# Output-map products of an S5 layer moved from GpSimd to VectorE inside a hidden-layer MLP stage

## The chip, the cores and the metric

The kernel runs on one core of one Trainium2 chip. The time is the device time of one execution in microseconds (us); lower is better. The engines are TensorE (PE, with its weight loads as PEld), VectorE (DVE), ScalarE (ACT), GpSimd (POOL) and SyncE (SP), whose queue issues nearly all DMA transfers. Each engine takes its own instructions strictly in their order.

## The reference, cut to what matters

A sequence of 256 tokens of width 1024 runs through two blocks of two layers each, in float32. The first block ends with a stick-breaking attention and an MLP (`x + gate * relu(h w1)^2 w2`, hidden width 4096). The second block begins with an S5 layer, a diagonal state-space model in 64 groups of 16 channels with 64 complex states each:

```
lam_bar = jnp.exp(lam * dt)
b_bar = ((lam_bar - 1.0) / lam)[..., None] * b
bu = jnp.einsum('blgc,gpc->blgp', uf, b_bar)
_, states = lax.associative_scan(_ssm_binop, (a_elems, bu), axis=1)
y = jnp.real(jnp.einsum('blgp,gcp->blgc', states, c))
```

The kernel computes the S5 layer in pieces of 8 tokens. For that it needs, of each group of channels, an input map P (powers of `lam_bar` times `b_bar`), an output map K (powers of `lam_bar` times `c`) and a band of the local response (the product of the two). All three depend on the weights alone, and the kernel makes them on the chip before the S5 layer begins.

## The kernel before, in words

Weights are split into two parts that TensorE takes at full rate: ScalarE copies a 1 MB unit `raw` (128x2048) to `wh`, and VectorE writes `wl = raw - wh`. The splitting is done by `unit_ahead` (`act` is line 292, `tt` line 312), and two such units are needed for each step of an MLP.

The MLP of the first block's second layer (tag `m2`, the stage named mlp1 in the code) has 16 units of 256 hidden columns. Step u consists of `A(u)`, 48 matmuls that give hidden unit u in two PSUM banks, then VectorE's `wb` and `ht`, ScalarE's relu, square and `hh` copy, VectorE's `hl = ht - hh`, and of `B(u-1)`, 48 matmuls that multiply the unit before with w2. Banks 0 to 3 hold the output; the pairs 4, 5 and 6, 7 take turns for `A`.

Between these blocks the function `mlp` calls `sides(b)` twice a step: once behind `A(u)`, once behind `B(u-1)`. Each call advances three generators by a bit, and lends them the bank pair that `A` doesn't hold: `ada_side` (dot products for the modulation, line 668), `s5_turns` (angle tables, written to DRAM through SP) and `s5_pre2`, which makes the maps. `s5_pre2` treats 8 blocks b of 8 groups:

- `maps(b)`: three VectorE instructions of 128x1024 make P (`s5A`, with `tP` in `s5X` as scratch), three GpSimd instructions of 128x1152 (`gp`, line 1358) make K (`s5X`); then SP loads the coefficients of block b+2 (line 1357) and stores K (`dQ`).
- `turn(b, h)`, h = 0 and 1: TensorE turns four groups of P into the first lent bank, ScalarE copies it out (`s5X<-psall`), SP stores it (`dP`); four matmuls of P with K fill 128 columns of the second lent bank, which VectorE copies to `s5Kp` (line 1395). After h = 1 VectorE adds the diagonal to `s5Kp` and SP stores it in four pieces (`dK`).

The generator's order before is: one call with `maps(b)` and `turn(b-1, 0)`, the next with `turn(b-1, 1)` alone. The order of POOL and SP is the program's; the order of DVE, ACT and PE in this stage is set by a scheduler when the kernel is built. A matmul must wait until the bank that it writes has been emptied.

Of the kernel before, what the change touches and what calls it, by code (L numbers as in the profile page):

```python
# [10 lines left out]
F32 = mybir.dt.float32  # L11
F32R = mybir.dt.float32r
U8 = mybir.dt.uint8
AF = mybir.ActivationFunctionType
# [9 lines left out]
D = 1024  # L24
NK = D // 128
# [13 lines left out]

S5SEQ = "g P0 P1 g T0 T1 TB0 M0 P2 P3 TB1 Q0 Q1 T2 T3 g Q2 Q3"


# [227 lines left out]
class Prog:  # L272
# [122 lines left out]
    def unit_ahead(self, ahead, between=None):  # L395

        last = min(self.used_n + ahead, len(self.wseq) - 1)
        while self.split_n <= last:
            j = self.wseq[self.split_n]
            if j not in self.slot:  # L400
                assert self.split_n > self.used_n, ("not loaded", self.plan[j][1])
                break
            b = self.split_n % len(self.hb)
            raw = self.raw_of(j)
            n = 1 + (self.plan[j][1][0] in HALVES)
            parts = [slice(i * 2048 // n, (i + 1) * 2048 // n) for i in range(n)]
            for c in parts:
                self.act(self.hb[b][:, c], raw[:, c], AF.Copy)
            if between is not None:
                between()  # L410
                between = None
            for c in parts:
                self.tt(self.lb[b][:, c], raw[:, c], self.hb[b][:, c].bitcast(F32), SUB)
            self.release(j)
            self.split_n += 1
        if between is not None:
            between()
# [76 lines left out]
                wh, wl = (t[:, k, m * 128:(m + 1) * 128] for t in (hv, lv))  # L494
                self.pair(outs[m], wh, wl, self.X2[S][:, k], k == 0, k == NK - 1)

    def rows_mm(self, units, xs, banks, start, stop, evac=None):

        kt = [(h, l, j) for h, l in units for j in range(2)]
        out = lambda m: self.pb[banks[m // 2]][:, (m % 2) * T:(m % 2 + 1) * T]  # L500
        if evac is not None:
            fin, a, b = evac
        for m in range(NK):
            o = out(m)
            for q, (h, l, j) in enumerate(kt):
                c = j * D + m * 128
                xh, xl = xs[q]
                wh, wl = h[:, c:c + 128], l[:, c:c + 128]
                self.mm(o, wh, xh, q == 0 and start and m % 2 == 0, False)
                self.mm(o, wh, xl, False, False)  # L510
                self.mm(o, wl, xh, False, q == len(kt) - 1 and stop and m % 2 == 1)
            if evac is not None and m % 2 == 1:
                for i in (m - 1, m):
                    fin(i, out(i))
                    a(i)
                    if i:
                        b(i - 1)
        if evac is not None:
            b(NK - 1)
# [412 lines left out]
    def mlp(self, tag, S, finish, side=(), after=None, before=None):  # L932
        n = DFF // 256
        with self.tc.tile_pool(name="pm" + tag, bufs=1) as p:
            hh = [p.tile([128, 2, T], F32R, name=f"hh{i}") for i in range(3)]
            hl = [p.tile([128, 2, T], F32R, name=f"hl{i}") for i in range(3)]
            tt_ = [p.tile([128, 2, T], F32, name=f"ht{i}") for i in range(2)]
            wb = [p.tile([128, 2], F32, name=f"wb{i}") for i in range(2)]
            yb = (0, 1, 2, 3)

            def A(u):
                b = 4 + 2 * (u % 2)
                t = s = tt_[u % 2]
                ps = [self.pb[b], self.pb[b + 1]]
                self.proj_T((tag + "a", u), S, ps, n=258, parts=1 + (u == 0))
                if u == 0:
                    self.stats(6, std=True, r2=True)
                w = wb[u % 2]
                self.red(w, self.pball[:, b:b + 2, 256:258], ADD)
                for m in range(2):  # L950
                    self.stt(t[:, m, :], self.stdb, w[:, m:m + 1], ps[m][:, :T], MUL, ADD)
                self.act(t, t, AF.Relu)
                self.act(s, t, AF.Square)
                self.act(hh[u % 3], s, AF.Copy)
                self.tt(hl[u % 3], s, hh[u % 3].bitcast(F32), SUB)

            def B(us, fin=None):
                ws = [self.unit((tag + "b", u), ahead=2 - i) for i, u in enumerate(us)]
                xs = [(hh[u % 3][:, j, :], hl[u % 3][:, j, :]) for u in us for j in range(2)]
                self.rows_mm(ws, xs, yb, us[0] == 0, us[-1] == n - 1, fin)  # L960

            def sides(b):
                self.side_banks = (b, b + 1)
                for g, budget in side:
                    start = self.vcost
                    while next(g, "end") == "more" and self.vcost - start < budget:
                        pass

            A(0)
            for u in range(1, n - 1):  # L970
                A(u)
                sides(6 - 2 * (u % 2))
                if u == n - 2:
                    A(n - 1)
                B([u - 1])
                sides(4 + 2 * (u % 2))
            for g, _ in side:
                for _ in g:
                    pass
            if after is not None:  # L980
                after()
            if before is not None:
                before()
            B([n - 2, n - 1], finish)
# [348 lines left out]
    def s5_pre2(self):  # L1333

        nc = self.nc
        with self.tc.tile_pool(name="s5s", bufs=1) as p:
# [18 lines left out]
            dd = self.rsb.rearrange("p (g c) -> p g c", c=16)  # L1355
            nc.sync.dma_start(out=self.rsb, in_=self.a["s5d"])
            load = lambda b: nc.sync.dma_start(out=blk[b % 2], in_=self.a["s5blk"][b].rearrange("p a (s c) -> p a s c", c=16))
            gp = lambda out, a, b, op: nc.gpsimd.tensor_tensor(out=out, in0=a, in1=b, op=op)  # L1358
            nc.gpsimd.memset(Kp, 0.0)
            for i in range(2):  # L1360
                load(i)
            for _ in range(5):
                yield

            def maps(b):
                v, P, K = blk[b % 2], Pt[b % 2], Kt[b % 2]
                sl = slice(8 * b, 8 * b + 8)
                co = lambda i, k: v[:, i, :, None, :].to_broadcast([128, 8, k, 16])
                wv = lambda t, k: t[:, :, sl].rearrange("p d (s o) -> p s d o", o=1).to_broadcast([128, 8, k, 16])
                self.tt(P, co(0, 8), wv(WR, 8), MUL)  # L1370
                self.tt(tP, co(1, 8), wv(WI, 8), MUL)
                self.tt(P, P, tP, ADD)
                gp(K, co(2, 9), wv(X1, 9), MUL)
                gp(tK, co(3, 9), wv(X2, 9), MUL)
                gp(K, K, tK, ADD)
                if b < 6:
                    load(b + 2)
                nc.sync.dma_start(out=self.dram["Q"][b // 2][:, (b % 2) * 1024:(b % 2 + 1) * 1024]
                                  .rearrange("p (s x) -> p s x", x=128),
                                  in_=K[:, :, 1:9, :].rearrange("p s d c -> p s (d c)"))  # L1380

            def turn(b, h):
                P, K = Pt[b % 2], Kt[b % 2]
                b0, b1 = self.side_banks
                for s in range(4):
                    self.tr(self.pb[b0][:, s * 128:(s + 1) * 128], P[:, 4 * h + s, :, :].rearrange("p d c -> p (d c)"))
                self.act(Pu, self.pb[b0].rearrange("p (s x) -> p s x", x=128), AF.Copy)
                o = (b % 2) * 1024 + h * 512
                nc.sync.dma_start(out=self.dram["P"][b // 2][:, o:o + 512], in_=Pu.rearrange("p s x -> p (s x)"))
                for q in range(4):  # L1390
                    s = 4 * h + q
                    self.mm(self.pb[b1][32 * q:32 * q + 32, 0:128], P[:, s, 6:8, :].rearrange("p d c -> p (d c)"),
                            K[:, s, 0:8, :].rearrange("p d c -> p (d c)"))
                kp = Kp
                nc.vector.tensor_copy(out=kp[:, h, 112:240], in_=self.pb[b1][:, 0:128])
                if h:
                    self.tt(kp[:, :, 112:128], kp[:, :, 112:128], dd[:, 2 * b:2 * b + 2, :], ADD)
                    kd = self.dram["K"][:, b * 1920:(b + 1) * 1920].rearrange("p (g q x) -> p q g x", q=4, x=240)
                    for q in range(4):
                        nc.sync.dma_start(out=kd[:, q], in_=kp[32 * q + 16:32 * q + 32])  # L1400

            for b in range(9):
                if b < 8:
                    maps(b)
                if b:
                    turn(b - 1, 0)
                    yield
                    turn(b - 1, 1)
                yield

    def s5_turn(self, m):
# [394 lines left out]
```

## Time and profile before

| | |
|---|---|
| time, 3 runs | 1330.76 us median (1329.8 to 1332.6) |
| profiled execution | 1333.17 us |
| its span, first to last instruction | 1331.4 us |
| mean granted TensorE clock | 0.972 |
| stretch in which the maps are made | 514 to 681 us |

The profile is of a single execution. "Busy" is the time in which an engine has an instruction under way; a wait row names the engine and line that waited, and what ended the wait. Of the 1333.17 us, 1.77 us lie outside the span.

### The profile page before, as it was taken

How to read it: one execution, taken by the hardware profiler on the slowest of the kernel's cores; microseconds unless marked ns; L12 is line 12 of the kernel's file. 1: busy time of each engine (PE TensorE's matmuls, PEld its weight loads, DVE VectorE, ACT ScalarE, POOL GpSimd, SP SyncE). 2: the span in 40 equal slices, each digit the busy share in tenths (PEclk: the TensorE clock that was granted, in tenths of full speed). 3: DMA queues.
4: the chain of work that ended last, by engine and by line, in shares of the span. 5: the costliest groups of instructions: out<-in, count | busy, mean ns of one | idle time of the engine just before them, and what ended most of it. 6: DMA issues, size and time to landing. Idle time of an engine off the chain costs nothing.

```text
span 1331.4 us, 22520 instructions
## 1 busy us (share of the span) xinstructions
PE 1234.0 (93%) x9412; PEld 1144.7 (86%) x9412; DVE 1043.7 (78%) x1390; ACT 678.5 (51%) x868; POOL 169.2 (13%) x97
## 2 busy tenths in 40 slices
PE   2999999999999997977899789999999999999997
PEld 2999999999988897966889669887889999988886
DVE  6899999985999979898966856667656786877553
ACT  4545465554558855433455425544445555655442
POOL 0013110000200025145610203100000000100000
PEclk7999999999999999978999989999999999999999
DMA  9776567777365545847579795444555532455520
GB/s 384 311 276 261 238 232 266 280 285 286 136 246 220 225 182 200 298 166 236 179 228 244 239 271 229 175 171 166 218 187 200 204 132 96 158 190 190 197 88 32
DMA packets 63654, 283.84 MB, mean 213 GB/s; under 512 B 8000, under 2 KB 25920, under 8 KB 31936
## 3 DMA queue, kind: packets, MB, share of 16 engines
q1 hardware_dynamic: 63552, 282.40, 59.9%
q8 instruction: 74, 1.21, 0.4%
q14 instruction: 28, 0.23, 0.1%
HBM read 267.70 MB, written 14.68 MB: 212 GB/s over the span
## 4 chain that ended last, share of the span: by engine, by line
PE 63%; DVE 20%; ACT 7%; issue 5%; DMA 3%; POOL 1%; DVEq 0%; ACTq 0%; POOLq 0%; SPq 0%
PE psall L335 62%; DVE wl L312 7%; ACT wh L292 4%; DVE raw L668 3%; DMA raw<-dK 2%; DVE s5A L312 1%; PE psall L338 1%; DMA raw<-in_wst_dram 1%; DVE tmpn L325 1%; DVE sqt L312 1%; DVE sqt L325 1%; DVE hl L312 1%; DVE X L325 1%; DVE td L312 1%; POOL sqat L546 1%
## 5 line engine op out<-in xcount | busy, mean ns | idle before, releaser
L335 PE MATMUL psall<-X,wh 128*128 128x256 f32 (+2 forms) x3360 | 733.4, 309 | 40.8 <-ACT wh L292 24.4
L335 PEld LDWEIGHTS psall<-X,wh 128*128 128x128 f32 x3360 | 548.2, 193 | 79.6 <-ACT wh L292 25.0
L335 PE MATMUL psall<-X,wl 128*128 128x256 f32 (+1 forms) x1992 | 561.3, 285 | 13.5 <-DVE wl L312 13.5
L312 DVE TENSOR_TENSOR wl<-raw,wh 128x2048 fp32r<-128x2048 f32 (+1 forms) x232 | 437.3, 1902 | 114.8 <-ACT wh L292 114.4
L292 ACT ACTIVATE wh<-raw 128x2048 fp32r<-128x2048 f32 (+1 forms) x232 | 354.3, 1546 | 223.1 <-PE psall L335 200.2
L335 PEld LDWEIGHTS psall<-X,wl 128*128 128x128 f32 x1992 | 379.8, 191 | 19.9 <-DVE wl L312 19.1
L546 POOL TENSOR_TENSOR sqat<-sqat,sqt 128x256 f32<-128x256 f32 x52 | 56.3, 1082 | 903.2 <-ACT sqt L292 902.1
L335 PE MATMUL psall<-hl,wh 128*128 128x256 f32 x512 | 146.5, 287 | 4.0 <-DVE hl L312 4.0
L335 PE MATMUL psall<-hh,wh 128*128 128x256 f32 x512 | 145.6, 289 | 4.6 <-ACT hh L292 4.6
L335 PE MATMUL psall<-hh,wl 128*128 128x256 f32 x512 | 145.8, 286 | 0.0
L335 PE MATMUL psall<-hid,wh 128*128 128x512 f32 (+1 forms) x432 | 136.4, 372 | 0.0
L335 PE MATMUL psall<-hid,wl 128*128 128x256 f32 x384 | 108.0, 281 | 0.2 <-DVE wl L312 0.2
L335 PEld LDWEIGHTS psall<-hh,wh 128*128 128x128 f32 x512 | 98.4, 194 | 7.3 <-ACT hh L292 5.6
L335 PEld LDWEIGHTS psall<-hl,wh 128*128 128x128 f32 x512 | 99.6, 195 | 5.0 <-DVE hl L312 4.4
L335 PEld LDWEIGHTS psall<-hh,wl 128*128 128x128 f32 x512 | 99.5, 194 | 0.6 <-issue 0.6
L335 PEld LDWEIGHTS psall<-hid,wh 128*128 128x128 f32 x432 | 78.1, 189 | 15.5
L668 DVE CUSTOM_DVE_ANT_0 raw<-raw,adaacc,prmt 128x1024 f32<-128x1024 f32 x64 | 81.2, 1291 | 0.0
L335 PEld LDWEIGHTS psall<-hid,wl 128*128 128x128 f32 x384 | 72.6, 189 | 0.5 <-DVE wl L312 0.5
L1358 POOL TENSOR_TENSOR s5X<-s5X,s5WX 128x1152 f32<-128x1152 f32 x16 | 55.8, 3509 | 86.5 <-PE psall L335 70.0
L292 ACT ACTIVATE ht<-ht 128x512 f32<-128x512 f32 x64 | 40.0, 626 | 29.3 <-DVE ht L325 28.5
L292 ACT ACTIVATE tmpn<-psall 128x256 f32<-128x256 f32 (+1 forms) x38 | 17.7, 467 | 62.2 <-PE psall L335 62.2
L312 DVE TENSOR_TENSOR tmpn<-tmpn,psall 128x256 f32<-128x256 f32 (+1 forms) x32 | 17.6, 552 | 38.0 <-ACT tmpn L292 38.0
(345 smaller groups left out, 1313.5 us busy)
## 6 DMA issues: line engine op xcount, KB each, us to landing
raw<-in_wst_dram SPq DMA_DIRECT2D x231, 1024.0 KB, 5.0
dQ<-s5X SPq DMA_DIRECT2D x8, 512.0 KB, 8.3
dP<-s5X SPq DMA_DIRECT2D x16, 256.0 KB, 3.9
s5X<-in_wst_dram SPq DMA_DIRECT2D x4, 1024.0 KB, 14.1
raw<-dK SPq DMA_DIRECT2D x32, 128.0 KB, 9.3
s5X<-in_s5blk_dram SPq DMA_DIRECT2D x8, 256.0 KB, 6.4
s5X<-dP SPq DMA_DIRECT2D x2, 1024.0 KB, 10.1
raw<-dP SPq DMA_DIRECT2D x2, 1024.0 KB, 12.5
```

Source lines behind the costliest of these rows:

```text
L292: i = self.nc.scalar.activation(out=out, in_=in_, func=func, **kw)
L312: return self.nc.vector.tensor_tensor(out=out, in0=a, in1=b, op=op)
L325: return self.nc.vector.scalar_tensor_tensor(out=out, in0=a, scalar=s, in1=b, op0=op0, op1=op1)
L335: return self.in_bank(out, self.nc.tensor.matmul(out, lhsT=l, rhs=r, start=start, stop=stop))
L338: return self.in_bank(out, self.nc.tensor.transpose(out, in_, self.ident))
L546: self.nc.gpsimd.tensor_tensor(out=self.sqa, in0=self.sqa, in1=s, op=ADD)
L668: self.nc.vector.tensor_tensor_reduce(out=w, in0=w, in1=self.crow, scale=1.0 if sc is None else sc, scalar=b, op0=MUL, op1=ADD, accum_out= ...
L1358: gp = lambda out, a, b, op: nc.gpsimd.tensor_tensor(out=out, in0=a, in1=b, op=op)
```

## The change

K is made by VectorE (`tt`) in place of GpSimd. The making of P becomes a function `ins(b)`, and a block's work is spread over two calls: one with `turn(b-1, 0)` and then `ins(b)`, the next with `turn(b-1, 1)` and then `maps(b)`, which now makes K alone. So `turn(b, h)` stands one call (half a step of the MLP) later than before. ScalarE instead of VectorE copies the band's bank to `s5Kp`.

```
-            gp = lambda out, a, b, op: nc.gpsimd.tensor_tensor(out=out, in0=a, in1=b, op=op)
...
+            def ins(b):
+                P = Pt[b % 2]
+                self.tt(P, co(b, 0, 8), wv(b, WR, 8), MUL)
+                self.tt(tP, co(b, 1, 8), wv(b, WI, 8), MUL)
+                self.tt(P, P, tP, ADD)
             def maps(b):
...
-                gp(K, co(2, 9), wv(X1, 9), MUL)
-                gp(tK, co(3, 9), wv(X2, 9), MUL)
-                gp(K, K, tK, ADD)
+                K = Kt[b % 2]
+                self.tt(K, co(b, 2, 9), wv(b, X1, 9), MUL)
+                self.tt(tK, co(b, 3, 9), wv(b, X2, 9), MUL)
+                self.tt(K, K, tK, ADD)
...
-                nc.vector.tensor_copy(out=kp[:, h, 112:240], in_=self.pb[b1][:, 0:128])
+                self.act(kp[:, h, 112:240], self.pb[b1][:, 0:128], AF.Copy)
...
             for b in range(9):
-                if b < 8:
-                    maps(b)
-                if b:
-                    turn(b - 1, 0)
-                    yield
-                    turn(b - 1, 1)
+                if b:
+                    turn(b - 1, 0)
+                if b < 8:
+                    ins(b)
+                yield
+                if b:
+                    turn(b - 1, 1)
+                if b < 8:
+                    maps(b)
                 yield
```

The diff also adds an empty table `DMALO` and two branches that ask for it (in `unit_ahead` and `rows_mm`); with the table empty neither is ever taken.

VectorE, one step of the MLP in the middle of the stage, before (`s5A` is P, `s5X` the scratch of P, `s5Kp` the band):

```order
L312 TENSOR_TENSOR s5A<-s5X,s5WX 128x1024
L312 TENSOR_TENSOR wl_76<-raw_68,wh_73 128x2048
L312 TENSOR_TENSOR hl_4778<-ht_4781,hh_4775 128x512
L1395 COPY s5Kp<-psall 128x128 x2
L312 TENSOR_TENSOR s5A<-s5A,s5X 128x1024
L312 TENSOR_TENSOR s5Kp<-s5Kp,rsbt 128x2x16
L312 TENSOR_TENSOR s5X<-s5X,s5WX 128x1024
L332 TENSOR_REDUCE wb_4784<-psall 128x2
L325 SCALAR_TENSOR_TENSOR ht_4782<-stdbt,wb_4784,psall 128x256 x2
L312 TENSOR_TENSOR wl_77<-raw_69,wh_74 128x2048
```

and of the change (rows of 128x1152 are K and its scratch):

```order
L314 TENSOR_TENSOR s5Kp<-s5Kp,rsbt 128x2x16
L314 TENSOR_TENSOR s5A<-s5X,s5WX 128x1024
L314 TENSOR_TENSOR s5X<-s5X,s5WX 128x1024
L314 TENSOR_TENSOR s5X<-s5X,s5WX 128x1152
L314 TENSOR_TENSOR s5A<-s5A,s5X 128x1024
L314 TENSOR_TENSOR s5X<-s5X,s5WX 128x1152
L314 TENSOR_TENSOR s5X<-s5X 128x1152
L334 TENSOR_REDUCE wb_4784<-psall 128x2
L327 SCALAR_TENSOR_TENSOR ht_4782<-stdbt,wb_4784,psall 128x256 x2
L314 TENSOR_TENSOR wl_77<-raw_69,wh_74 128x2048
```

Both copies of the band's bank have left VectorE, and three instructions of 128x1152 have come in ahead of `wb` and `ht`.

ScalarE, the same part of the stage, before (`ht` is relu and square of a hidden unit, `s5X<-psall` the copy of turned P):

```order
L292 ACTIVATE s5X<-psall 128x512
L292 ACTIVATE ht_4782<-ht_4782 128x512 x2
L292 ACTIVATE hh_4775<-ht_4782 128x512
L292 ACTIVATE wh_73<-raw_68 128x2048
L292 ACTIVATE s5X<-psall 128x512
```

and of the change:

```order
L294 ACTIVATE wh_75<-raw_70 128x2048
L294 ACTIVATE s5X<-psall 128x512
L294 ACTIVATE ht_4782<-ht_4782 128x512
L294 ACTIVATE s5Kp<-psall 128x128
L294 ACTIVATE ht_4782<-ht_4782 128x512
L294 ACTIVATE s5Kp<-psall 128x128
L294 ACTIVATE hh_4775<-ht_4782 128x512
L294 ACTIVATE wh_73<-raw_68 128x2048
L294 ACTIVATE s5X<-psall 128x512
```

The two copies of the band's bank stand between relu, square and `hh` of a hidden unit.

SP's queue, around the load of the last block's coefficients (`s5X<-in_s5blk_dram`), before:

```order
L376 DMA raw_69<-in_wst_dram 128x2048
L1389 DMA dP<-s5X 128x512
L1400 DMA dK<-s5Kp 16x2x240 x4
L376 DMA raw_72<-in_wst_dram 128x2048
L1357 DMA s5X<-in_s5blk_dram 128x512
L1378 DMA dQ<-s5X 128x8x128
```

and of the change (`dTB` and `dM` are stores of the angle tables from VectorE's and ScalarE's work):

```order
L378 DMA raw_71<-in_wst_dram 128x2048
L1350 DMA dTB<-tmpn 128x512
L1350 DMA dTB<-sqt 128x512
L1350 DMA dM<-adaacc_135 128x512
L1411 DMA dP<-s5X 128x512
L1422 DMA dK<-s5Kp 16x2x240 x4
L1377 DMA s5X<-in_s5blk_dram 128x512
L1400 DMA dQ<-s5X 128x8x128
```

The stores of a set of tables now stand ahead of `dP`, `dK` and that load; the same happens at the load for the third block.

## Rows read from the trace of the kernel before

**Rows 1.** Page, parts 1 and 2: busy us of each engine; POOL's share by 40 slices.
```profile
PE 1234.0 (93%) x9412; PEld 1144.7 (86%) x9412; DVE 1043.7 (78%) x1390; ACT 678.5 (51%) x868; POOL 169.2 (13%) x97
...
POOL 0013110000200025145610203100000000100000
```

**Rows 2.** Stretches: length, busy us (instructions) PE, PEld, DVE, ACT, POOL; clock, DMA.
```profile
514.00:681.00 167.00, 134.35 (x1040) 126.18 (x1040) 155.32 (x140) 68.18 (x72) 84.92 (x24) 0.89 0.63 205
681.00:704.00 23.00, 23.00 (x202) 22.30 (x201) 11.26 (x17) 14.95 (x17) 0.00 (x0) 1.00 0.76 247
```

**Rows 3.** Chain that ended last, 514 to 731: start, us, what ran.
```profile
632.01 8.13 PE psall L335 x57
...
659.66 4.35 DVE wl L312
...
690.25 40.63 PE psall L335 x343
```

**Rows 4.** Waits of PE, 514 to 681: us in total, times, longest.
```profile
PE psall L335 <- DVE s5Kp L1395: 11.4, 4, 3.7
PE psall L335 <- DVE wl L312: 7.9, 1, 7.9
PE psall L335 <- ACT hh L292: 4.6, 3, 1.6
```

**Rows 5.** Timeline of POOL: start us, us, instruction, count.
```profile
528.47 4.57 POOL L1358 TENSOR_TENSOR s5X<-s5X 128x1152 f32<-128x1152 f32 x1
...
560.71 5.47 POOL L1358 TENSOR_TENSOR s5X<-s5X,s5WX 128x1152 f32<-128x1152 f32 x2 [27.67 <-PE psall L335]
```

**Rows 6.** Timeline of DVE, the same columns.
```profile
526.22 4.33 DVE L312 TENSOR_TENSOR wl<-raw,wh 128x2048 fp32r<-128x2048 f32 x1
...
537.03 2.28 DVE L312 TENSOR_TENSOR wl<-raw,wh 128x2048 fp32r<-128x2048 f32 x1
...
560.67 0.29 DVE L1395 COPY s5Kp<-psall 128x128 f32<-128x128 f32 x1 [1.71 <-PE psall L335]
...
563.99 2.25 DVE L312 TENSOR_TENSOR s5Kp<-s5Kp,rsbt 128x32 f32<-128x32 f32 x1
```

**Rows 7.** Groups of DVE, 514 to 681: count, busy us, mean ns, idle before.
```profile
L312 DVE TENSOR_TENSOR wl<-raw,wh 128x2048 fp32r<-128x2048 f32 x19 | 54.4, 2865 | 3.5 <-ACT wh L292 3.5
L312 DVE TENSOR_TENSOR s5A<-s5A,s5X 128x1024 f32<-128x1024 f32 x8 | 17.9, 2242 | 0.0
L312 DVE TENSOR_TENSOR s5A<-s5X,s5WX 128x1024 f32<-128x1024 f32 x8 | 14.2, 1777 | 3.4 <-PE psall L335 3.4
L312 DVE TENSOR_TENSOR s5X<-s5X,s5WX 128x1024 f32<-128x1024 f32 x8 | 13.8, 1729 | 0.0
L312 DVE TENSOR_TENSOR hl<-ht,hh 128x512 fp32r<-128x512 f32 x9 | 10.2, 1136 | 0.0
...
L312 DVE TENSOR_TENSOR s5Kp<-s5Kp,rsbt 128x32 f32<-128x32 f32 x6 | 7.7, 1285 | 0.0
...
L1395 DVE COPY s5Kp<-psall 128x128 f32<-128x128 f32 x14 | 3.4, 279 | 1.7 <-PE psall L335 1.7
```

**Rows 8.** The same groups, 681 to 704, where POOL has nothing.
```profile
L312 DVE TENSOR_TENSOR wl<-raw,wh 128x2048 fp32r<-128x2048 f32 x3 | 6.9, 2292 | 2.5 <-ACT wh L292 2.5
...
L312 DVE TENSOR_TENSOR hl<-ht,hh 128x512 fp32r<-128x512 f32 x2 | 1.4, 688 | 0.0
...
L312 DVE TENSOR_TENSOR s5Kp<-s5Kp,rsbt 128x32 f32<-128x32 f32 x2 | 0.4, 192 | 0.1
```

**Rows 9.** Tile s5X: ns least/median/most of one, first and last start.
```profile
L312 DVE TENSOR_TENSOR s5A<-s5X,s5WX x8: 1209/1224/3711, 519.4 to 658.5; 128x1024 f32<-128x1024 f32 x8
```

**Rows 10.** Whole span, group of ACT that copies 128x128 from PSUM.
```profile
L292 ACT ACTIVATE fp<-psall,fmx 128x128 f32<-128x128 f32 x16 | 5.9, 369 | 15.8 <-DVE fmx L332 15.8
```

**Rows 11.** Line 1357, loads of coefficient blocks: time from issue to landing.
```profile
DMA to landing us min/median/max: 5.6/6.4/9.6
```

**Rows 12.** Timeline of SP: the four dK stores of one block.
```profile
569.29 1.78 SPq L1400 DMA_DIRECT2D dK<-s5Kp  x4
```

More of the change, by code (lines that the diff above doesn't have):

```diff
@@ L38 @@
 ROUND = 12582912.0
+DMALO = ()
 S5SEQ = "g P0 P1 g T0 T1 TB0 M0 P2 P3 TB1 Q0 Q1 T2 T3 g Q2 Q3"
@@ L404, in unit_ahead @@
             raw = self.raw_of(j)
+            if self.plan[j][1] in DMALO:
+                self.act(self.hb[b], raw, AF.Copy)
+                self.release(j)
+                lo = self.lb[b]
+                self.act(lo, self.hb[b].bitcast(F32), AF.Copy, scale=-1.0)
+                self.nc.gpsimd.dma_start(out=lo, in_=self.a["wst"][self.wpos[j]], accum_op=ADD)
+                self.split_n += 1
+                continue
             n = 1 + (self.plan[j][1][0] in HALVES)
@@ L495, in proj_2, with rows_mm @@
                 self.pair(outs[m], wh, wl, self.X2[S][:, k], k == 0, k == NK - 1)
-    def rows_mm(self, units, xs, banks, start, stop, evac=None):
+    def rows_mm(self, units, xs, banks, start, stop, evac=None, late=False):
         kt = [(h, l, j) for h, l in units for j in range(2)]
@@ L502, in rows_mm @@
             fin, a, b = evac
+        if late:
+            for q, m in [(q, m) for q in range(2) for m in range(NK)]:
+                h, l, j = kt[q]
+                w = h[:, j * D + m * 128:j * D + (m + 1) * 128]
+                self.mm(out(m), w, xs[q][0], q == 0 and start and m % 2 == 0, False)
+                self.mm(out(m), w, xs[q][1], False, False)
+            for q, m in [(q, m) for q in range(2) for m in range(NK)]:
+                h, l, j = kt[q]
+                self.mm(out(m), l[:, j * D + m * 128:j * D + (m + 1) * 128], xs[q][0], False, q == 1 and stop and m % 2 == 1)
+            return
         for m in range(NK):
@@ L959, in B @@
                 xs = [(hh[u % 3][:, j, :], hl[u % 3][:, j, :]) for u in us for j in range(2)]
-                self.rows_mm(ws, xs, yb, us[0] == 0, us[-1] == n - 1, fin)
+                self.rows_mm(ws, xs, yb, us[0] == 0, us[-1] == n - 1, fin, (tag + "b", us[0]) in DMALO)
             def sides(b):
@@ L1363, in s5_pre2 @@
                 yield
-            def maps(b):
[L1366 to L1372, printed above, removed]
-                gp(K, co(2, 9), wv(X1, 9), MUL)
-                gp(tK, co(3, 9), wv(X2, 9), MUL)
-                gp(K, K, tK, ADD)
+            co = lambda b, i, k: blk[b % 2][:, i, :, None, :].to_broadcast([128, 8, k, 16])
+            wv = lambda b, t, k: t[:, :, 8 * b:8 * b + 8].rearrange("p d (s o) -> p s d o", o=1).to_broadcast([128, 8, k, 16])
+            def ins(b):
[3 more added lines that the diff above has]
+                self.tt(P, P, tP, ADD)
+            def maps(b):
+                K = Kt[b % 2]
+                self.tt(K, co(b, 2, 9), wv(b, X1, 9), MUL)
+                self.tt(tK, co(b, 3, 9), wv(b, X2, 9), MUL)
+                self.tt(K, K, tK, ADD)
                 if b < 6:
```

## The prediction

> **What bounds the kernel now.** I read the page first, then the busy times by stretch, the chain that ended last, the waits, and then single instructions. Over the whole span TensorE is busy 93%, VectorE 78% and POOL 13% [rows 1], which says nothing yet: the change touches only the stretch from 514 to 681 us, where POOL's digits rise. There TensorE is busy 134 of 167 us at a granted clock of 0.89, and VectorE 155 of 167. In the 23 us behind it POOL has nothing to do, TensorE is busy all the time at 1.00, and VectorE is half idle [rows 2]. So one stage has two regimes: VectorE bounds it while maps are made, TensorE afterwards. TensorE's own need in the first regime follows from the second: 23.00 us / 202 = 0.114 us a matmul, and 1040 of them make 118.6 us. Some 48 us of the 167 are therefore lost to waiting and to the clock, between the 1.2 GHz and 2.4 GHz levels on average.
>
> The chain shows the same. It changes between VectorE's pieces (a `wl` of 4.35 us) and TensorE's pieces (57 matmuls in 8.13 us, 0.143 each); from 690 us it is TensorE alone, 343 matmuls in 40.63 us, 0.118 each [rows 3]. TensorE waits most for VectorE's copy of the band's bank, then for `wl`, then for ScalarE's `hh` [rows 4], which itself needs VectorE's `ht`.
>
> **What GpSimd costs VectorE.** This is the term on which the forecast rests. The same `wl` of 128x2048 takes 4.33 us at 526 us, with POOL's products running beside it [rows 5], and 2.28 us at 537 us without them: 2.05 us more. An addition to 32 columns of `s5Kp` takes 2.25 us beside a product at 564 us, and 0.19 us later [rows 6, 8], again 2.06 more. The copy from PSUM at 560.67 us lies beside a product too and takes its usual 0.29 us [rows 5, 6]. So a product holds up an instruction of VectorE that reads SBUF twice, by about 2.05 us, and POOL makes 24 products in the stretch [rows 2]: 24 x 2.05 = 49.2 us. From the groups: what each took in the stretch less its count times the undisturbed duration is 10.9 us for `wl` (54.4 - 19 x 2.29), 8.2, 4.5 and 4.1 for the three of P (at 1.21 each), 4.0 for `hl` and 6.6 for `s5Kp` [rows 7 to 9]. That is 38.3 us in six kinds, and the angle tables' instructions hold the rest. I take 48, with 38 and 49 as bounds.
>
> The Trainium skill's page "SBUF — State Buffer", section "Who interferes with whom", states that a VectorE instruction with two SBUF inputs contends with a GpSimd instruction that reads SBUF, that one with a single SBUF input does not, and that whoever comes first keeps the port for its whole instruction. On which instructions are held this trace agrees (the copy from PSUM is untouched at 0.29 us); on how long, it shows 2.05 us, where a product lasts 84.92 / 24 = 3.5 us on average. By whole instructions the removal would be worth up to 85 us instead of 48, and the sum would stop only at TensorE's bound, 1333.2 - 48 - 2.4 = 1283 us; the rows bear that out so little that it has 0.01, within rival 2.
>
> **The change, part by part.**
>
> *Products on VectorE.* 24 instructions of 128x1152, which the trace doesn't show on VectorE. 128x1024 takes 1.21 us and 128x2048 2.29 us, so 128 more columns cost 0.135 us: 1.345 us each, 32.3 us in all [rows 8, 9]. The operands are spread over an axis as those of P are, so no other price seems near; the least is that of P, 24 x 1.21 = 29.
>
> *Holds gone.* -48 us as above.
>
> *The bank's copy goes to ScalarE.* 14 copies in the stretch free 3.4 us of VectorE [rows 7]. On ScalarE the nearest row, a 128x128 read from PSUM with another function, is 0.37 us [rows 10]; 16 of them make 6 us on an engine that is busy 68 of 167 us [rows 2]. I charge nothing. That cover is by share only: the order puts two copies between relu, square and `hh` of a hidden unit, so they can hold `hh`; this is the third rival.
>
> *Net on VectorE.* 48 + 3.4 - 32.3 = 19 us less, 136 instead of 155 us.
>
> *Half a step later.* The last `turn` moves by one call, so 48 matmuls (5.5 us) that came behind the stretch now run within it, with one more `wl` and half of a hidden unit's `wb`, `ht` and `hl`, about 3.2 us on VectorE. Since VectorE bounds there: 5.5 - 3.2 = 2.3 us gained.
>
> *SP's queue.* The coefficients of the third and the last block now stand behind the stores of a set of tables, which wait for VectorE's own table work. In the last case `dM`, `dP`, four `dK` (1.8 us of issuing, [rows 12]) and the load itself come to some 3 us, and landing takes 6.4 us, 9.6 at most [rows 11], while VectorE's work between the table's last write and the first use of those coefficients is by my estimate about 8 us (a `wl` of 2.3, an `hl` of 0.7, ten small ones at some 0.5). So VectorE can miss them by 1 to 5 us; the third block's place is similar. I charge 2 us for both together, with 0 and 10 as bounds. What is queued behind is each time the next weight unit, four or more units ahead of its use. The S5 stage behind reads `dK` and `dP` half a step later than before, but TensorE's 40.6 us of MLP matmuls lie in between [rows 3]: charged at nothing; without that cover at most 5.5 us.
>
> *What stays.* VectorE idles 167.0 - 155.3 = 11.7 us in the stretch, for `wh` and for TensorE [rows 7]. I keep it. The 11.4 us that TensorE waits for the bank's copy are not counted apart: they lie where VectorE, too, was late.
>
> *Sum.* 19 + 2.3 - 2 = 19.3, rounded to 20 since TensorE's pieces in the chain speed up a little with a better clock. The profiled execution took 1333.17 us, of which 1331.4 are its span; with 20 less it would take 1313.2. It stands 2.4 above the median of the runs shown, 1330.76, so the median to expect is 1311.
>
> **The rivals.**
>
> *1. The chain tightens.* VectorE's 136 us, with the half step 139, and TensorE's 118.6 + 5.5 = 124 come close, and three products of 4 us in all now stand in a row ahead of `wb` and `ht`. Then each engine waits for the other more often. If VectorE's idle time doubles and a bit, from 12 to 26 us, the gain shrinks to 20 - 14 = 6: 1325 us. For it: TensorE already waits for `hh` and `wl` at full VectorE [rows 4]. Against it: before, three of P, two `wl` and held instructions also stood ahead of `wb`, at 18.6 us a step (nine `hl` in 167 us, [rows 7]).
>
> *2. Everything meshes.* The waits for the bank's copy vanish, the clock comes back to 1.00, and VectorE works without idling: 167 + 5.5 - 139 = 33.5 us gained, 1297 us. TensorE alone would allow 48, 1283. For it: in the stretch without POOL the clock is 1.00 at once [rows 2].
>
> *3. Slower: ScalarE's queue holds `hh`.* The second copy needs matmuls that write the same bank as the first, so they wait for the first copy, which stands behind relu, which needs `ht`. Also the first copy of a block may write `s5Kp` only when the `dK` stores of the block before have landed. Both waits delay `hh`, `hl` and the next `B`. The price is bounded by nothing below, and above by what stands between: 1.8 us of issuing, some 2 us of landing and a `wl` of 2.3 us that VectorE may do before it adds the diagonal, 6 us a block. It decides from (20 + 2.7) / 8 = 2.8 us a block; at 4 us a block the time is 1311 + 32 = 1343. Against it: half a step, 5.5 us of TensorE's work, lies between the two calls, and ScalarE idles more than half of the stretch.
>
> *4. It doesn't do what it says.* If VectorE's long instructions were not GpSimd's doing, it would gain 32 - 3 us of work: about 1360. Every row argues against it.
>
> **How the numbers follow.** The forecast with its surroundings (1303 to 1319) gets 0.56; rival 2 0.16; rival 1 0.15 (of which a third within 0.2%); rival 3 0.12, not all of it slower; rival 4 0.01. About 0.2%, 2.7 us, is what a measurement of this kernel can tell from no change. Faster is then 0.56 + 0.16 + 0.10 + 0.03 = 0.85, the same 0.06, slower 0.09. The range goes from rival 2's end, 1297, to rival 1's, 1325; left out are rival 3's worse half, rival 4, and a part of either end, 0.2 in all. The likeliest case alone: 1303 to 1319.
>
> **What would show it.** In the new profile POOL has no products between 500 and 700 us; `wl` there takes 2.3 us and the additions to `s5Kp` 0.19 us, with none near 4.3 and 2.2. The 24 products take 1.35 us each on VectorE. A step of the MLP takes 16 to 17 us instead of 18.6. TensorE's clock in the stretch lies above 0.89, and no wait for `s5Kp` stands near 11 us. The stage's end comes some 20 us earlier and nothing behind it changes. I am wrong if TensorE's waits for `hh` or for ScalarE's copy of `s5Kp` grow above some 20 us, if VectorE shows idle time for the coefficients, or if holds remain without GpSimd.

## The result, and the profile after

The changed kernel takes 1311.41 us (median of 4 runs, 1310.66 to 1315.48), the kernel before 1330.28 us beside it (1327.4 to 1332.6): a ratio of 0.9864, 95% interval 0.984 to 0.9888, or 18.9 us less. The prediction was 1311, with 20 us less. The profiled execution took 1311.48 us, with a span of 1309.7 against 1331.4.

The page of the changed kernel: busy us and share of each engine, POOL's share by 40 slices, and the chain that ended last.

```profile
PE 1225.6 (94%) x9412; PEld 1138.2 (87%) x9412; DVE 1021.1 (78%) x1398; ACT 681.8 (52%) x884; POOL 85.5 (7%) x73
...
POOL 0012120000100001000000204000000000100000
...
PE 68%; DVE 16%; ACT 8%; DMA 4%; issue 3%; POOL 1%; DVEq 0%; ACTq 0%; SPq 0%; POOLq 0%
```

POOL has lost its 24 products, and its digits in slices 16 to 21 have gone from 514561 [rows 1] to 100000. Two stretches, with the columns of [rows 2]: the one in which the maps are made, and a piece of the end of the MLP.

```profile
514.00:665.00 151.00, 133.09 (x1090) 126.94 (x1089) 136.72 (x151) 75.77 (x88) 0.00 (x0) 0.93 0.66 226
665.00:690.00 25.00, 23.13 (x203) 21.68 (x203) 10.44 (x13) 11.64 (x16) 0.00 (x0) 1.00 0.84 279
```

In 151 us TensorE now issues 1090 matmuls where it had 1040 in 167, and the granted clock is 0.93 instead of 0.89, still between the 1.2 and 2.4 GHz levels. VectorE is busy 137 us and idle 14. Its groups from 514 to 665 us, with count, busy us, mean ns and idle time before them as in [rows 7]:

```profile
L314 DVE TENSOR_TENSOR wl<-raw,wh 128x2048 fp32r<-128x2048 f32 x20 | 45.7, 2287 | 2.2 <-ACT wh L294 2.2
L314 DVE TENSOR_TENSOR s5X<-s5X,s5WX 128x1152 f32<-128x1152 f32 x16 | 21.5, 1352 | 0.0
L314 DVE TENSOR_TENSOR s5X<-s5X 128x1152 f32<-128x1152 f32 x8 | 10.8, 1354 | 0.1
...
L314 DVE TENSOR_TENSOR hl<-ht,hh 128x512 fp32r<-128x512 f32 x9 | 6.2, 686 | 0.6 <-ACT hh L294 0.6
...
L314 DVE TENSOR_TENSOR s5Kp<-s5Kp,rsbt 128x32 f32<-128x32 f32 x6 | 1.1, 188 | 0.4 <-ACT s5Kp L294 0.4
```

Every kind is back at the duration that [rows 8] show without POOL: `wl` 2.29 us instead of 2.87 on average, `hl` 0.69 instead of 1.14, the additions to `s5Kp` 0.19 instead of 1.29. Counting each VectorE instruction between 505 and 705 us that runs over 0.3 us longer than the shortest of its kind, I find 24 of them and 48.8 us of excess before, and none after. The waits of the same stretch, in us, times and longest:

```profile
ACT s5X L294 <- DMA dP<-s5X: 16.1, 7, 5.1
...
PE psall L337 <- ACT s5X L294: 9.8, 2, 7.4
DVE wb L334 <- PE psall L337: 9.1, 2, 7.5
...
PE psall L337 <- ACT hh L294: 4.3, 1, 4.3
...
PE psall L337 <- ACT s5Kp L294: 2.6, 3, 1.8
```

TensorE's wait for the band's copy has fallen from 11.4 us [rows 4] to 2.6, and that for `wl` is gone. What has come in its place is ScalarE's copy of turned P. ScalarE waits 16.1 us for the store `dP` of the copy before to land, since there is one buffer `Pu`. How much of TensorE's 9.8 us that explains, the rows don't tell: the longest of its waits, 7.4 us, ends with a copy that also stood behind an angle-table instruction in ScalarE's order.

Where in the stage the time comes from is seen in the start of ScalarE's `hh` copy of a hidden unit u: start in the kernel before less start in the other kernel, in us.

| | u = 5 | 6 | 8 | 11 | 15 |
|---|---|---|---|---|---|
| changed kernel | 20.0 | 17.5 | 27.4 | 20.3 | 19.7 |
| products on VectorE alone | 18.6 | 1.6 | 11.5 | 3.7 | 4.0 |
| the same, stores from GpSimd's queue | 17.3 | 30.5 | 42.7 | 21.8 | 17.7 |
| changed, two buffers for P and band | 19.2 | 32.3 | 33.3 | 28.8 | 28.2 |
| changed, without K's products | 20.7 | 32.3 | 46.5 | 47.8 | 47.4 |

In the changed kernel the gain reaches 27 us in the middle, and about 8 are given back before the MLP ends. From there on the difference stays at 20 to 22 us. The other rows belong to the experiments.

### The profile page after: what moved, and what is told of

Same layout as the page of the kernel before. It is cut to its first block, busy times and chain, and to the rows that moved or that the text cites. A ratio compares the mean times of both kernels' runs of the same rounds, so it can differ in the third digit from the quotient of the medians.

```text
span 1309.7 us, 22500 instructions
## 1 busy us (share of the span) xinstructions
PE 1225.6 (94%) x9412; PEld 1138.2 (87%) x9412; DVE 1021.1 (78%) x1398; ACT 681.8 (52%) x884; POOL 85.5 (7%) x73
## 4 chain that ended last, share of the span: by engine, by line
PE 68%; DVE 16%; ACT 8%; DMA 4%; issue 3%; POOL 1%; DVEq 0%; ACTq 0%; SPq 0%; POOLq 0%
PE psall L337 67%; DVE wl L314 6%; ACT wh L294 5%; DVE raw L688 2%; DMA raw<-dK 2%; DMA raw<-in_wst_dram 1%; PE psall L340 1%; DMA raw<-dP 1%; DVE tmpn L327 1%; DVE sqt L327 1%; DVE X L327 1%; DVE td L314 1%; POOL sqat L566 1%; DVE sqt L314 0%; ACT X L294 0%
## 5 line engine op out<-in xcount | busy, mean ns | idle before, releaser
L314 DVE TENSOR_TENSOR wl<-raw,wh 128x2048 fp32r<-128x2048 f32 (+1 forms) x232 | 426.6, 1856 | 108.7 <-ACT wh L294 108.3
L337 PEld LDWEIGHTS psall<-X,wl 128*128 128x128 f32 x1992 | 378.0, 190 | 12.1 <-DVE wl L314 11.3
L294 ACT ACTIVATE tmpn<-psall 128x256 f32<-128x256 f32 (+1 forms) x38 | 17.7, 465 | 62.1 <-PE psall L337 62.1
L314 DVE TENSOR_TENSOR tmpn<-tmpn,psall 128x256 f32<-128x256 f32 (+1 forms) x32 | 17.6, 552 | 38.0 <-ACT tmpn L294 38.0
L688 DVE CUSTOM_DVE_ANT_0 raw<-raw,adaacc,adn 128x1024 f32<-128x1024 f32 x32 | 42.3, 1340 | 4.4 <-ACT td L294 4.4
```

The costliest lines, as they stand in the source:

```text
L294: i = self.nc.scalar.activation(out=out, in_=in_, func=func, **kw)
L314: return self.nc.vector.tensor_tensor(out=out, in0=a, in1=b, op=op)
L337: return self.in_bank(out, self.nc.tensor.matmul(out, lhsT=l, rhs=r, start=start, stop=stop))
L688: self.nc.vector.tensor_tensor_reduce(out=w, in0=w, in1=self.crow, scale=1.0 if sc is None else sc, scalar=b, op0=MUL, op1=ADD, accum_out= ...
```

## Experiments

Each edit also changes the order that the scheduler builds for VectorE, ScalarE and TensorE, so that a few us of any difference may come from that order. The ratios are against the kernel before, run beside each; where kernels of different sets are compared, the difference of medians stands first and that by the ratios (times 1330 us) behind it.

**1. The products alone.** The kernel before with `gp` replaced by `self.tt`; order of the calls and bank copy as before.

```
-                gp(K, co(2, 9), wv(X1, 9), MUL)
-                gp(tK, co(3, 9), wv(X2, 9), MUL)
-                gp(K, K, tK, ADD)
+                self.tt(K, co(2, 9), wv(X1, 9), MUL)
+                self.tt(tK, co(3, 9), wv(X2, 9), MUL)
+                self.tt(K, K, tK, ADD)
```

> The kernel before with one edit: the 24 K products run on VectorE; the order of the calls and VectorE's copy of the band's bank stay. Theory of the holds (a GpSimd product holds a VectorE instruction with two SBUF inputs by about 2.05 us; that is what the change removes): nearly the whole gain of 19 us, 1310 to 1318 us, no instruction of VectorE in the stretch stretched, TensorE's waits for the copy of the bank partly left. Theory of the order (the half step and the copy on ScalarE make the gain, and the products on VectorE cost): 1330 us or above, up to 1330 + 32 = 1362.

Measured: 1329.31 us, ratio 0.9984 (0.9968 to 1.0001). All 48.8 us of holds are gone, as in the changed kernel, and nearly nothing is gained: the theory that the holds carry the gain by themselves fell. The table shows where it goes: 17 us are lost between units 5 and 6. There SP's own waits, and the timeline of its queue (start, us, line, transfer, count), have

```profile
SPq L1330 <- DVE adaacc L1330: 22.0, 1, 22.0
SPq L376 <- DVE mod L668: 15.1, 1, 15.1
```

```profile
565.22 0.52 SPq L1389 DMA_DIRECT2D dP<-s5X  x1
565.78 16.68 SPq L376 DMA_DIRECT2D raw<-in_wst_dram  x2
582.56 0.38 SPq L1389 DMA_DIRECT2D dP<-s5X  x1
583.03 2.08 SPq L1400 DMA_DIRECT2D dK<-s5Kp  x4
```

that of ScalarE

```profile
571.64 0.60 ACT L292 ACTIVATE s5X<-psall 128x512 f32<-128x512 f32 x1 [9.41 <-DMA dP<-s5X]
...
584.74 0.63 ACT L292 ACTIVATE tmpn<-sqt 128x512 f32<-128x512 f32 x1 [9.16 <-DVE sqt L321]
...
589.50 0.60 ACT L292 ACTIVATE s5X<-psall 128x512 f32<-128x512 f32 x1 [1.47 <-DMA dP<-s5X]
```

and that of VectorE

```profile
580.81 1.28 DVE L668 CUSTOM_DVE_ANT_0 raw<-raw,adaacc,prmt 128x1024 f32<-128x1024 f32 x1
...
590.17 0.49 DVE L1395 COPY s5Kp<-psall 128x128 f32<-128x128 f32 x2 [5.46 <-DMA dK<-s5Kp]
```

SP first stands 22 us at the store of an angle table that VectorE delivers late; the first half of block 0's P, copied out at 542.4, goes only at 565.2. Then SP stands from 566 to 582 us at the second of two weight loads, whose buffer becomes free when VectorE's dot product of `ada_side` has read it at 582.1. The other stores of block 0 stand behind it: the second half of its P goes out at 582.6, its band at 583. So the next copy of P finds `Pu` taken, the next copy of the band finds `s5Kp` taken, TensorE finds no empty bank, and one wait of 17.1 us is the longest of this kernel:

```profile
PE psall L335 <- ACT s5X L292: 20.7, 3, 17.1
```

Only the last 1.5 us of it are ScalarE's wait for `dP` itself. Before that ScalarE waited 9.2 us for an angle table (`sqt`), which VectorE, busy without a break from 573 to 584.7, wrote last, and worked on it for 3.3 us; the copy of P stands behind both in ScalarE's order. Whether the late stores or the order of the calls is the cause can't be read from this trace. Experiments 5 and 6 ask it.

**2. The bank's copy alone** (before, with `self.act(kp[:, h, 112:240], ...)` for `tensor_copy`; GpSimd keeps the products).

> The kernel before with one edit: ScalarE copies the band's bank; products stay on GpSimd, the order of the calls stays. Holds: VectorE loses 4.5 us of copies and TensorE's 11.4 us of waits for it shrink, but the 24 holds stay: 1323 to 1329 us. Order: much of the gain, 1312 to 1322.

Measured: 1338.11 us, ratio 1.0047 (1.0032 to 1.0062), with 24 holds of 51.8 us. Alone this part costs 7 us (6 by the ratio), and neither expectation held. TensorE's 11.4 us of waits for the band's copy are gone, but it waits 12.1 us longer for ScalarE's copy of P, which stands in two of the three places behind ScalarE's wait for angle tables that VectorE, still held up, delivers late. That wait of ScalarE's is about as long as before (24.8 us there). Where the 7 us come from is not shown beyond this. The waits of this kernel, and the second of them in the kernel before:

```profile
ACT tmpn L292 <- DVE sqt L321: 25.3, 3, 12.7
...
PE psall L338 <- ACT s5X L292: 15.6, 3, 6.4
```

```profile
PE psall L338 <- ACT s5X L292: 3.5, 2, 2.2
```

**3. Spreading and bank copy, products back on GpSimd** (the changed kernel with `gp` in `maps`).

> The changed kernel with the K products back on GpSimd: half step and copy on ScalarE stay. Holds: 24 stretched instructions come back, 1322 to 1330 us. Order: as the changed kernel, 1309 to 1315.

Measured: 1325.81 us, ratio 0.9963 (0.9946 to 0.9979); 22 holds, 44.2 us. The time lies in the range that the expectation of the holds gave. The two parts are worth 5 us without the third. TensorE waits for the band's copy and for `wl`, as before the change:

```profile
PE psall L337 <- ACT s5Kp L294: 13.6, 3, 5.2
PE psall L337 <- DVE wl L314: 7.9, 1, 7.9
```

**4. GpSimd additions that nobody needs.** The changed kernel with 24 unread additions on GpSimd, three behind each block's K; to make room, `tP` shares the place of `tK`.

```
+                for _ in range(3):
+                    nc.gpsimd.tensor_tensor(out=spare, in0=K[:, :, 0:8, :], in1=K[:, :, 1:9, :], op=ADD)
```

> The changed kernel, and behind each K three additions of 128x1024 on GpSimd whose results nobody reads (24 in all; to make room P's scratch shares that of K). Nothing waits for them but the overwriting of K two blocks later. Holds: 24 x 2.05 = 49 us more on VectorE (185 us with the rest, so VectorE bounds again): 1335 to 1355 us, one hold of about 2.05 us for each product. No contention (before it was waiting that cost): 1309 to 1314.

Measured: 1352.44 us, ratio 1.0151 (1.0127 to 1.0176), 41.0 us above the changed kernel (38 by the ratios). Its groups of POOL (whole span) and of VectorE (514 to 700 us):

```profile
L1400 POOL TENSOR_TENSOR s5X<-s5X 128x1024 f32<-128x1024 f32 x24 | 80.3, 3344 | 132.5 <-DVE s5X L314 131.2
```

```profile
L314 DVE TENSOR_TENSOR wl<-raw,wh 128x2048 fp32r<-128x2048 f32 x20 | 54.3, 2716 | 1.6 <-ACT wh L294 1.6
...
L314 DVE TENSOR_TENSOR hl<-ht,hh 128x512 fp32r<-128x512 f32 x9 | 12.6, 1402 | 0.0
...
L314 DVE TENSOR_TENSOR tmpn<-s5t,cstt 128x512 f32<-128x512 f32 x3 | 6.4, 2140 | 0.0
```

Nothing waits for these additions' results, yet `wl` is at 2.72 us again, `hl` at 1.40, and a `tmpn` that takes 0.68 us undisturbed at 2.14. There are 21 holds with 41.4 us of excess up to 705 us (23 with 44.5 us when the last additions, which lie behind that, are counted), and the time is 38 to 41 us longer. GpSimd beside VectorE is the cause of the holds, and in this order of the calls one us of hold costs nearly one us of time.

How long a hold lasts is seen where VectorE and GpSimd meet (POOL, then DVE, of this kernel):

```profile
655.69 4.32 POOL L1400 TENSOR_TENSOR s5X<-s5X 128x1024 f32<-128x1024 f32 x1
660.09 2.73 POOL L1400 TENSOR_TENSOR s5X<-s5X 128x1024 f32<-128x1024 f32 x1
```

```profile
653.78 3.98 DVE L314 TENSOR_TENSOR wl<-raw,wh 128x2048 fp32r<-128x2048 f32 x1
657.68 2.88 DVE L314 TENSOR_TENSOR hl<-ht,hh 128x512 fp32r<-128x512 f32 x1
660.49 2.38 DVE L314 TENSOR_TENSOR s5Kp<-s5Kp,rsbt 128x32 f32<-128x32 f32 x1
```

Each of these additions starts beside an instruction of VectorE and ends 2.25 us after that one has ended (`wl` at 657.76, the addition at 660.01; `hl` at 660.56, the next at 662.82). The instruction of VectorE that began meanwhile ends right behind it: `hl`, 0.69 us by itself, 0.55 us later, and `s5Kp`, 0.19 us by itself, 0.05 us later. So the two engines take turns by whole instructions, each waits for the other, and the 4.32 and 2.73 us of these additions contain their own waiting.

**5. The other two pairs.** The changed kernel with VectorE's bank copy (products and spreading), and experiment 1 with ScalarE's bank copy (products and copy).

> The changed kernel with VectorE, not ScalarE, copying the band's bank: products on VectorE and work spread over two calls, without the third part. Theory (products and spreading carry the gain; the bank's copy is worth only its 4 us of VectorE time): 1310 to 1317. Rival (the bank's copy on VectorE is what TensorE waited for, 11 us before, and it comes late behind the products): 1319 to 1328.

> The kernel before with K's products on VectorE and ScalarE copying the band's bank, but in the order of calls of before (both steps of P and K in one call). Theory (the order of calls decides, since turn(b,0) comes too soon behind the maps and SP's queue is blocked then): 1325 to 1335, no better than the products alone. Rival (products and bank copy are what is needed, the spreading is worth little): 1311 to 1318.

Measured: products and spreading 1316.32 us, ratio 0.9892 (0.9876 to 0.9907); products and copy 1325.88, ratio 0.9963 (0.995 to 0.9977). Both theories hold. Spreading the work is what lets the products pay: 13.0 us (12 by the ratios) between 1329.31 and 1316.32 without ScalarE's copy, 14.5 (13) between 1325.88 and 1311.41 with it. The copy is worth 3 to 5 us once the products have left GpSimd.

**6. Is it SP's queue?** Three kernels on top of experiment 1, in the order of calls of before: two buffers for turned P, used in turns (the second in the place of `tP`, which moves onto `tK`); besides that two for the band; and, with single buffers, the stores `dP` and `dK` issued from GpSimd's queue.

```
-            Pu = self.s5X[:, 5504:6016].rearrange("p (s x) -> p s x", x=128)
+            Pus = [self.s5X[:, o:o + 512].rearrange("p (s x) -> p s x", x=128) for o in (5504, 1024)]
...
-                nc.sync.dma_start(out=self.dram["P"][b // 2][:, o:o + 512], ...
+                nc.gpsimd.dma_start(out=self.dram["P"][b // 2][:, o:o + 512], ...
```

> The kernel before with K's products on VectorE and two buffers for turned P; the order of the calls and VectorE's copy of the band's bank stay as before. Theory (what ate the gain of the products alone is the single buffer of turned P, whose store stands behind blocked weight loads in SP's queue): most of the gain returns, 1311 to 1319. Rival (it was the order of the calls itself: six map instructions of VectorE in one call and both turns behind them, and the buffer only showed it): 1325 to 1331, as with the products alone.

> The kernel before with K's products on VectorE, two buffers for turned P and two for the band (s5Kp); the order of the calls and VectorE's bank copy as before. With two buffers of turned P alone, VectorE's copy into the band still waited 7.0 us at one place for the dK stores of the block before, which stood in SP's queue behind two weight loads that were blocked for 15.4 us. Theory (what eats the gain of the products is that queue, through the buffers that its late stores hold): 1310 to 1316, no wait for dK, and the loss of 13 us between the hidden units 21 and 22 mostly gone. Rival (the order of the calls costs by itself, since both turns of a block come right behind its maps): 1318 to 1325, as with two buffers of P.

> The kernel before with K's products on VectorE, single buffers, order of calls as before, but the stores of turned P and of the band (dP, dK) are issued from GpSimd's queue, which has nothing else to do in this stage, in place of SP's. Theory (the stores are late because they stand behind blocked weight loads in SP's queue): the 15 to 17 us wait at the first turns goes, 1311 to 1318. Rival (they are late for another reason, or GpSimd's issuing costs as much, by holds on VectorE for instance): 1322 to 1331.

Measured: two P buffers 1321.46 us, ratio 0.9928 (0.9911 to 0.9944), between the two expectations; two P and two band buffers 1315.63, 0.9893 (0.9879 to 0.9907); the stores on the other queue 1313.16, 0.9874 (0.986 to 0.9887). The last two bring what spreading brings, without it. With two P buffers the queue is still blocked: TensorE's longest wait, 12.5 us, again ends with ScalarE's copy of P, and the band's buffer is missed too, as the timeline of VectorE shows:

```profile
588.56 0.49 DVE L1395 COPY s5Kp<-psall 128x128 f32<-128x128 f32 x2 [6.99 <-DMA dK<-s5Kp]
```

With the second band buffer I expected no wait for `dK`; one of 7.3 us was left, a block later, so that point was wrong. The clearest case is the other queue. SP stands still even longer, at weight loads alone:

```profile
566.77 21.91 SPq L376 DMA_DIRECT2D raw<-in_wst_dram  x3
```

and GpSimd sends the stores meanwhile:

```profile
567.95 2.03 POOL L1400 DMA_DIRECT2D dK<-s5Kp  x4 [2.75 <-DVE s5Kp L312]
571.37 0.59 POOL L1389 DMA_DIRECT2D dP<-s5X  x1 [1.39 <-ACT s5X L292]
578.11 0.56 POOL L1389 DMA_DIRECT2D dP<-s5X  x1 [6.16 <-ACT s5X L292]
```

At unit 6 the table has 30.5 us for it, where experiment 1 has 1.6. So that loss goes when the stores leave SP's queue: their place in it was the cause. How much of it was their late landing, and how much the order built around them, is not separated: in this kernel three copies of P stand ahead of the angle tables in ScalarE's order between 570 and 585 us, where experiment 1 has one. It isn't free: later on ScalarE waits 14.5 us between 598 and 640 for `dP` to land in the single buffer, and 42.7 us of gain shrink to 17.7.

**7. What bounds the changed kernel.** Two buffers for P; two for P and for the band; and K's products left out, but for the first multiplication of the first two blocks.

> The changed kernel with two buffers for turned P in turns (Pu), the second in the place of the scratch tP, which moves onto the scratch tK: VectorE alone writes both now. So ScalarE's copy of turned P no longer waits for the store of the copy before. Theory (what is left in the stage is ScalarE held by that store, 16 us of waiting in seven places, and TensorE behind it): the waits of s5X for dP go to about zero, and the time falls by 2 to 8 us below the changed kernel, 1303 to 1309. Rival (TensorE bounds the stage by now, and those waits are covered): within 2 us of the changed kernel, 1309 to 1314.

> The changed kernel with two buffers for turned P and two for the band. Theory (in the changed order the band's buffer is free in time, TensorE bounds): 1306 to 1311, within 2 us of two buffers of P alone. Rival (the waits that are left, 3 us for dK, count in full): 1302 to 1306.

> The changed kernel without K's products (only the first multiplication of the first two blocks is left, so the output isn't the reference's): 22 of 24 instructions and 29.7 us of VectorE work less. Theory (TensorE bounds the stage after the change, so VectorE's work is mostly covered): 3 to 10 us faster than the changed kernel, 1301 to 1308. Rival (VectorE still bounds, as before the change): 20 us or more faster, below 1291.

Measured: two P buffers 1309.43 us, ratio 0.9838 (0.9823 to 0.9853), whose interval overlaps that of the changed kernel: no gain is shown, as the rival had it. Two of each: 1302.92, ratio 0.9795 (0.9782 to 0.9808), 8.5 us (9) below the changed kernel, and faster than both kernels, as the rival had it (1302 to 1306). Without K's products: 1283.90, ratio 0.9658 (0.9645 to 0.9672). My theory there, that TensorE bounds by now, fell: 22 products, 22 x 1.352 = 29.7 us of VectorE's work, are worth 27.5 us (27) of time. (The edit also frees TensorE's matmuls with K from waiting for the products; what that is worth by itself is not shown.) The same stretch in the changed kernel, with two of each, and without the products:

```profile
514.00:650.00 136.00, 120.45 (x997) 114.84 (x996) 123.83 (x138) 69.23 (x80) 0.00 (x0) 0.94 0.66 224
```

```profile
514.00:650.00 136.00, 128.17 (x1084) 121.87 (x1083) 125.47 (x142) 70.37 (x83) 0.00 (x0) 0.97 0.67 230
```

```profile
514.00:650.00 136.00, 134.83 (x1183) 129.18 (x1182) 113.94 (x138) 82.25 (x97) 0.00 (x0) 1.00 0.84 278
```

Only in the last is TensorE busy all the time, at a clock of 1.00. In the changed kernel VectorE still has 91% of the stretch, though the chain lists mostly TensorE: its matmuls stand one behind the other at a clock of 0.94, and the chain names what ran, not what it was short of.

The kernel with two of each also bears on experiment 6. There the same buffers in the order of before, with VectorE's copy, gave 1315.63 us. The two differ by 12.7 us (13), which the spreading and ScalarE's copy are worth even with two buffers. ScalarE's waits for `dP` from 514 to 665 us, there and here, say that the buffers had not ended the collision in the order of before:

```profile
ACT s5X L292 <- DMA dP<-s5X: 17.5, 5, 10.0
```

```profile
ACT s5X L294 <- DMA dP<-s5X: 4.0, 1, 4.0
```

So the rival in experiment 6, that the order of the calls costs by itself, is not excluded.

## Why the prediction was right, and where it wasn't

**Holds gone, -48 us: right, by a reading that was wrong in part.** 48.8 us before, none after; experiment 4 puts 41.4 us of them back and loses 38 to 41 us. But the prediction set 2.05 us a hold against 3.5 us a product and took the hold for shorter than the instruction. The 3.5 us contain the product's own wait for VectorE. Counted from the end of the instruction of VectorE beside which it starts, a multiplication of the kernel before takes 2.12 us (median; 15 of the 16 lie between 2.02 and 2.14) and an addition 2.5 (2.49 to 2.55, all 8). So 24 products need some 54 us by themselves, not 85, and whole instructions and 48 us agree.

**Products on VectorE, 32.3 us: right.** 21.5 + 10.8 = 32.3 us in the groups. Experiment 7 shows that they count nearly in full.

**The bank's copy, 3.4 us freed and nothing charged: right in this order.** 0.27 us each on ScalarE, where the nearest row had 0.37; worth 4.9 us (4 by the ratios) against products and spreading alone. "I charge nothing. That cover is by share only" held here; in the order of before the same edit gains 3 us without holds (experiment 5 against 1) and costs 7 us with them (experiment 2).

**Half a step later and SP's queue, +2.3 and -2: the step that was mis-sized.** The prediction gave the spreading 0.3 us in all. It is worth 12 to 14.5. The sum of 20 still came out, because it took VectorE's time saved as time saved, and that is true only of an order in which nothing else is late. That the order of the change is nearly such a one is in part luck: of the half step the prediction said that it lies between two calls (rival 3), not that the gain needs it. With two buffers of each the same parts give 28 us (27 by the ratio). In the order of before the same sum, 48 - 32.3 = 15.7 us without the copy, came to 2; with the stores on another queue, or with two buffers of each, to 17.6 and 15.1. The prediction looked at what stands behind the stores in SP's queue (coefficients, weights) and not at the stores of P and the band standing behind weight loads and table stores that are themselves blocked. The coefficients that it charged 2 us for came in time: VectorE's waits from 505 to 735 us have no row for them. In the changed kernel SP stands still for as long,

```profile
553.75 15.66 SPq L378 DMA_DIRECT2D raw<-in_wst_dram  x2
569.50 0.38 SPq L1411 DMA_DIRECT2D dP<-s5X  x1
...
576.38 0.33 SPq L1411 DMA_DIRECT2D dP<-s5X  x1
576.80 1.79 SPq L1422 DMA_DIRECT2D dK<-s5Kp  x4
```

but only the first `dP` of block 0 is behind it. The second turn comes half a step later, ScalarE's next copy waits 0.5 us, and the `dK` stores go out at once. Whether the half step by itself, apart from that collision, gains 2.3 us or costs something was not measured.

**VectorE's idle time, 11.7 us kept: nearly right**, 14.3 in 151 us. The step of the MLP took 151 / 9 = 16.8 us, within the 16 to 17 forecast, and the clock rose to 0.93.

**The rivals.** The first, a tighter chain with 6 us of gain, and the third, `hh` held by the copies, didn't come: one wait for `hh` of 4.3 us, and 2.6 us for the copies. The second, everything meshes, stood at 1297; two buffers of each come nearest (1302.92), 8.5 us of the 14 that the changed kernel lacks. The bound of 1283 for TensorE alone is about what is left without the products (1283.90).

**By the Trainium skill**, page "SBUF — State Buffer", section "Who interferes with whom", a VectorE instruction with two SBUF inputs contends with a GpSimd instruction that reads SBUF. Experiment 4 agrees, with additions that share no data with the `wl` and `hl` that they hold up. The rule from that page that whoever comes first keeps the port for its whole instruction, which the prediction gave 0.01, agrees too: 2.25 us of an addition by itself, and 41.4 / 21 = 1.97 us a hold, since some instructions of VectorE start when much of the addition is done. The prediction left out a condition of the same section: that an instruction with one SBUF input doesn't contend holds only outside the modes in which VectorE uses both port pairs. The trace of the kernel before has three such instructions among its 24 holds, for one

```profile
647.57 2.08 DVE L321 TENSOR_SCALAR sqt<-sqt 128x512 f32<-128x512 f32 x1
```

which takes 0.42 us undisturbed; in which mode it ran, no row says.

## What to carry to other kernels

When work is moved off an engine that contends with the bottleneck, the time of the bottleneck that is saved can be read from the profile before, instruction by instruction. The duration of the other engine's instruction is no measure of it, since it contains that engine's own waiting. Whether it arrives depends on what the faster engine then runs into: look up, for each single buffer in the stage, which queue its store is in and what can block that queue. One test tells: give the stores another queue or, less plainly, the buffer a twin. A busy share of 91% beside a chain that lists another engine does not say which of the two bounds; leaving the work out does.

## What was not expected of the hardware

The holds go both ways, and their length is that of GpSimd's instruction alone, whatever VectorE's is: before the change, 1.7 to 2.1 us beside the 16 multiplications of 128x1152 (2.12 us by themselves) and 2.0 to 2.5 beside seven of the eight additions (2.5 by themselves; 0.4 beside the eighth, which was nearly over), for instructions of VectorE of 0.19 to 2.29 us. The 24 products are listed with 84.9 us; some 31 us of that are more than they need by themselves, spent beside instructions of VectorE. And GpSimd issuing 48 DMA transfers beside VectorE (0.51 us for one `dK`, 0.59 for a `dP`) held up no instruction of VectorE by more than 0.3 us.
